# Second down pair of a decoder layer: six of eleven chunks by seven products instead of three, with two weight sums of each made by DMA

## The chip, the cores and the metric

The kernel runs on one core of one Trainium2 chip. The metric is the device time of one execution in microseconds (us), lower is better. Times shown are medians of several runs, beside the lowest and the highest; one execution was also profiled, and all rows of the trace come from that one.

## What is computed

One layer of a decoder for 256 rows of 2048 numbers, in float32. The part that matters here is the last product of the feed-forward half, from 5632 to 2048 columns:

```python
    h2 = rmsnorm(x, g_ffn)
    gu = h2 @ w_gu
    x = x + (jax.nn.silu(gu[..., :D_FF]) * gu[..., D_FF:]) @ w_down
    return x
```

In the kernel the product of silu and the second half of `gu` is called `a`; it has 256 rows and 5632 columns, and is needed transposed.

## The kernel before

**Precision.** TensorE (PE) multiplies in a format shorter than float32. Each operand is therefore split: ScalarE (ACT) casts it to a high part (`w_hi`, `a_hi`), and VectorE (DVE) subtracts that from the original and keeps the rest as a low part (`w_lo`, `a_lo`). `split` (line 108) emits the two instructions. `product` (lines 170 to 172) then issues three matmuls, high by high, high by low, low by high, each 128x128 by 128x512. So each weight tile costs one ACT and one DVE instruction of 128x1024, and then PE uses it. `w_hi` and `w_lo` have five buffers each, the raw weights `w_raw` four.

**The down product.** `a` is cut into eleven chunks of 512 columns, the output into four blocks of 512 columns, and the blocks are made two at a time: `down_pair` is called twice, and each call makes 256 rows by 1024 columns. `own` holds its four PSUM tiles (row half t, column block n). A chunk gives each of the four a contribution. Plainly done (`rest`, one call for each column block n and half of the chunk kh) this takes four weight tiles, four splits and 48 matmuls.

**By sevens.** Three of the eleven chunks (`WD`, chunks 4, 6 and 8) are done by `seven` instead: the 2x2 block product of a chunk is made from seven products of sums, in the manner of Strassen and Winograd. The four weight tiles b11, b12, b21, b22 (`g_raw`, four buffers) are summed into `u` (one buffer) and into b12, and each of the seven `form` calls splits one tile and issues 6 matmuls: 42 for the chunk instead of 48. Sums of `a` are wanted too; `sums` makes them with four small DVE steps in place, and they are split into `a_shi` and `a_slo`. Four of the seven products collect in PSUM tiles of their own (`f1`, `f5`, `f6`, `f7`, from `spare`) over all the chunks done so, and `combine` adds them to the output once per pair.

**What sets the order.** `down_pair` calls `rest` for the plain chunks in turn and takes steps of the generator `by_sevens` between them. Each split also advances the queue `stages`, which brings in the chunks of `a`: `fetch_a` (line 1028) loads a chunk from DRAM (`a_mem`) into `a_raw`, two buffers, and `take_a` splits it. The order in which the program was written is then rearranged by a scheduler while it is built, so an engine's real row of instructions is read from its order, below. At run time each engine works through its row in that order.

**Queues.** Weight loads are issued by SyncE (SP, line 291), loads of `a_raw` and of the residual by GpSimd (POOL), outputs by two queues for each pair. An earlier stage, the product with `w_gu`, already has sums that are made by DMA: line 366, `u<-g_raw`, a DMA with `accum_op` add, issued by POOL, 512 KB.

Of the kernel before, what the change touches and what calls it, by code (L numbers as in the profile page):

```python
# [9 lines left out]
F32 = mybir.dt.float32  # L10
# [3 lines left out]
ALU = mybir.AluOpType  # L14
# [4 lines left out]
P = 128  # L19
D = 2048  # L20
S = 256
NT = S // P
# [7 lines left out]
NB = 512  # L30
# [25 lines left out]
def hybrid_block(ctx: ExitStack, tc: tile.TileContext, x, w_in, w_branch, w_out, w_gu, w_down, rel_bias,  # L56
                 onehot, extra, across, factors, out):
    nc = tc.nc
# [22 lines left out]
    def pool(stack, name, side, bufs=1):  # L81
        return stack.enter_context(tc.tile_pool(name=name, bufs=bufs, side=side, reuse_waits="tile"))
# [8 lines left out]
    def half_kb(dt=F32):  # L91

        return scratch.tile([P, NB], dt, name="sc")
# [13 lines left out]
    def split(hi, lo, src, pin=False):  # L107
        for op in nc.scalar.copy(hi, src), nc.vector.tensor_sub(lo, src, hi.bitcast(F32)):  # L108
            if pin:
                tc.keep_in_program_order(op)  # L110
# [5 lines left out]
    def raw_weights(w, row0, c, col0):  # L116
        raw = wpool.tile([P, 2, NB], F32, name="w_raw", bufs=4)
        return raw, nc.sync.dma_start(raw, block(w, row0 // P + c, col0))
# [12 lines left out]
    stages, slow_stages = [], []  # L131
# [35 lines left out]
    def product(ps, ah, al, wh, wl, start=False, stop=False):  # L167
        how = dict(skip_group_check=True)
        wh, wl = woven(wh), woven(wl)
        nc.tensor.matmul(ps, ah, wh, start=start, stop=False, **how)  # L170
        nc.tensor.matmul(ps, ah, wl, start=False, stop=False, **how)  # L171
        nc.tensor.matmul(ps, al, wh, start=False, stop=stop, **how)  # L172
# [36 lines left out]
    def sums(t0, t1, pin=False):  # L209


        a11, a12, a21, a22 = (a[:, 2 * kh:2 * kh + 2, :] for a in (t0, t1) for kh in range(2))
        first = nc.vector.tensor_sub(a22, a21, a22)
        if pin:
            tc.keep_in_program_order(first)
        nc.vector.tensor_sub(a21, a11, a21)
        nc.vector.tensor_sub(a11, a22, a11)
        nc.vector.tensor_add(a12, a12, a11)
# [3 lines left out]
    class Sums:  # L222
# [19 lines left out]
        def form(self, f, c, j):  # L242
            if f in SUM_AT:
                kh, t = SUM_AT[f]
                return [x[:, 2 * kh + j, t * P:(t + 1) * P] for x in self.s[c]]
            return self.plain(*{1: (0, 4 * c + j), 2: (0, 4 * c + 2 + j), 4: (1, 4 * c + 2 + j)}[f])
# [41 lines left out]
    def load(w, k, col0, pl=None):  # L288

        raw = pl.tile([P, 2, NB], F32, name="g_raw", bufs=6 if pl is gx else 4) if pl else wpool.tile([P, 2, NB], F32, name="w_raw", bufs=4)  # L290
        (nc.sync.dma_start if w is w_down else fetch)(raw, block(w, k, col0))
        return raw

    def parts(src):
        hi = wpool.tile([P, 2, NB], F32R, name="w_hi")
        lo = wpool.tile([P, 2, NB], F32R, name="w_lo")
        split(hi, lo, src)
        advance(stages)
        split_count[0] += 1
        if split_count[0] % 2:  # L300
            advance(slow_stages)
        return hi, lo
# [3 lines left out]
    def snapshot(ps):  # L306
        sb = half_kb()
        nc.scalar.copy(sb, ps)  # L308
        return sb
# [144 lines left out]
    for k in (4, 6):  # L454
        raw, issue = raw_weights(w_in, 0, k, V0)
# [497 lines left out]
    pr = pool(ctx, "pr", "right")  # L953
# [16 lines left out]
    a_mem = dram.tile([NF // 4, P, 4, S], F32, name="a_mem")  # L970

    WD = (4, 6, 8)
    ORDER = [0, 1, 2, 4, 3, 6, 5, 8, 7, 9, 10]
    EARLY = 3
    a = Chunks(None, "a", NF // 4, WD, False)
# [88 lines left out]

    stages.append(take_rest())

    def down_pair(c0, mine, spare, queues):


        own = dict(zip(((0, 0), (1, 0), (0, 1), (1, 1)), mine()))  # L1070
        begun = set()
        xc = {}
        for t in range(NT):
            for n in range(2):
                xc[t, n] = half_kb()
                nc.gpsimd.dma_start(xc[t, n], x1[t, :, c0 + n * NB:c0 + (n + 1) * NB])

        def into(ps, lhs, wh, wl, last=False):
            for j in range(2):
                product(ps, *lhs(j), wh[:, j], wl[:, j], id(ps) not in begun, last and j == 1)  # L1080
                begun.add(id(ps))

        def rest(c, n, kh, last=False):
            k = 4 * c + 2 * kh
            wh, wl = parts(load(w_down, k, c0 + n * NB))
            for t in range(NT):
                into(own[t, n], lambda j: a.plain(t, k + j), wh, wl, last)

        def form(ps, f, c, src, last=False):
            wh, wl = parts(src)  # L1090
            into(ps, lambda j: a.form(f, c, j), wh, wl, last)

        def seven(c, f1, f5, f6, f7, last):
            def quarter(kh, n):
                return load(w_down, 4 * c + 2 * kh, c0 + n * NB, gd)

            b11 = quarter(0, 0)
            form(f1, 1, c, b11, last)
            yield
            b12 = quarter(0, 1)  # L1100
            u = gd.tile([P, 2, NB], F32, name="u", bufs=1)
            tc.keep_in_program_order(nc.vector.tensor_add(u, b11, b12))
            form(f5, 5, c, u, last)
            yield
            b22 = quarter(1, 1)
            nc.vector.tensor_add(u, u, b22)
            form(f6, 6, c, u, last)
            yield
            nc.vector.tensor_add(b12, b12, b22)
            form(f7, 7, c, b12, last)  # L1110
            yield
            form(own[0, 1], 3, c, b22)
            yield
            b21 = quarter(1, 0)
            form(own[0, 0], 2, c, b21)
            yield
            nc.vector.tensor_add(u, u, b21)
            form(own[1, 0], 4, c, u)
            yield

        def combine(f1, f5, f6, f7):

            s1 = snapshot(f1)
            nc.vector.tensor_add(xc[0, 0], xc[0, 0], s1)
            nc.vector.tensor_add(s1, f6, s1)
            s3 = half_kb()
            nc.vector.tensor_add(s3, f7, s1)
            s5 = snapshot(f5)
            yield
            nc.vector.tensor_add(xc[1, 0], xc[1, 0], s3)  # L1130
            nc.vector.tensor_sub(s1, s5, s1)
            nc.vector.tensor_add(xc[0, 1], xc[0, 1], s1)
            nc.vector.tensor_sub(s3, s5, s3)
            nc.vector.tensor_add(xc[1, 1], xc[1, 1], s3)
            yield

        def by_sevens():
            f = spare()
            for c in WD:
                yield from seven(c, *f, c == WD[-1])  # L1140
            yield from combine(*f)

        sevens = by_sevens()
        plain = [(c, n, kh) for c in ORDER if c not in WD for kh in range(2) for n in range(2)]
        for i, at in enumerate(plain[:-4]):
            rest(*at)
            if i >= 6:
                next(sevens, None)
        for _ in sevens:
            pass  # L1150
        for n in range(2):
            for kh in range(2):
                rest(plain[-1][0], n, kh, kh == 1)
            for t in range(NT):
                for half in range(2):
                    n0 = half * (NB // 2)
                    cols = slice(n0, n0 + NB // 2)
                    y = xc[t, n]
                    nc.vector.tensor_add(y[:, cols], own[t, n][:, cols], y[:, cols])
                    queues[half].dma_start(  # L1160
                        out[t * P:(t + 1) * P, c0 + n * NB + n0:c0 + n * NB + n0 + NB // 2], y[:, cols])
# [4 lines left out]
    def elsewhere():  # L1166
        return [acc2.tile([P, NB], F32, name=n) for n in "zv"] + [tr.tile([P, NB], F32, name="tr") for _ in range(2)]

    down_pair(0, in_acc, elsewhere, (nc.scalar, nc.gpsimd))
    down_pair(2 * NB, elsewhere, in_acc, (nc.scalar, nc.sync))  # L1170


_INS = ["x", "w_in", "w_branch", "w_out", "w_gu", "w_down", "rel_bias"]
# [33 lines left out]
```

## Time and profile before

| | us |
|---|---|
| median of 3 runs (lowest, highest) | 1344.98 (1343.92, 1347.02) |
| profiled execution, its own time | 1344.12 |
| its span in the trace | 1342.4 |
| PE busy | 1333.9 |
| DVE busy | 1154.9 |
| ACT busy | 917.4 |
| POOL busy | 118.0 |

The span goes from the first instruction to the last; the execution's own time is a little longer. Busy time is the sum of the stretches in which an engine worked on an instruction. The records of matmuls overlap, so that the distance between the starts of two of them is the time that one takes.

### The profile page before, as it was taken

What the parts mean: (1) busy time and instruction counts of PE and PEld (TensorE: products, weight loads), DVE (VectorE), ACT (ScalarE), POOL (GpSimd) and SP (SyncE); (2) the same over time, 40 slices, a digit from 0 to 9 for tenths busy, and PEclk for the clock granted to TensorE, in tenths of its full rate; (3) what the DMA queues carried; (4) which work ended last, traced back from release to release, by engine and by line L of the source; (5) the groups of instructions that cost most, each with busy time, mean ns of one, the idle gap of its engine ahead of it and who ended that gap; (6) DMA issues with size and microseconds to landing.
All of it is one profiled execution on the core that took longest, in us unless ns stands there. A gap on an engine that the chain in (4) does not pass through costs nothing.

```text
span 1342.4 us, 17715 instructions
## 1 busy us (share of the span) xinstructions
PE 1333.9 (99%) x6266; PEld 1165.2 (87%) x6266; DVE 1154.9 (86%) x1239; ACT 917.4 (68%) x1175; POOL 118.0 (9%) x180
## 2 busy tenths in 40 slices
PE   9999999999999999999999999999999999999998
PEld 6888888888888888888888888888888888888887
DVE  7988898988889996876689999999999997996785
ACT  7786967888776775445567778777877876664453
POOL 1100010101110112100100000001000001000000
PEclk9999999999999999999999999999999999999999
DMA  9987877888788878977788989899999987787652
GB/s 361 305 282 248 268 208 246 269 255 244 250 276 278 268 241 286 309 232 223 238 325 258 269 250 282 222 263 302 289 281 284 245 240 254 251 307 239 204 186 96
DMA packets 117200, 346.83 MB, mean 258 GB/s; under 512 B 32576, under 2 KB 34296, under 8 KB 117112
## 3 DMA queue, kind: packets, MB, share of 16 engines
q1 hardware_dynamic: 76872, 277.45, 59.6%
q0 software_dynamic: 17824, 61.90, 19.7%
q10 hardware_dynamic: 22416, 6.36, 2.8%
q8 instruction: 49, 0.80, 0.2%
q14 instruction: 39, 0.32, 0.1%
HBM read 293.21 MB, written 14.70 MB: 229 GB/s over the span
## 4 chain that ended last, share of the span: by engine, by line
PE 96%; DVE 2%; ACT 1%; issue 0%; DMA 0%; SPq 0%; DVEq 0%; ACTq 0%
PE qs L171 12%; PE qs L170 12%; PE qs L172 12%; PE ps L171 12%; PE ps L172 12%; PE ps L170 12%; PE z L170 4%; PE z L171 4%; PE z L172 4%; PE v L171 2%; PE v L172 2%; PE v L170 2%; PE tr L172 1%; PE tr L170 1%; PE tr L171 1%; PE tr L192 1%
## 5 line engine op out<-in xcount | busy, mean ns | idle before, releaser
L108 DVE TENSOR_TENSOR w_lo<-w_raw,w_hi 128x1024 fp32r<-128x1024 f32 x318 | 386.9, 1221 | 86.2 <-ACT w_hi L108 84.6
L108 ACT CAST w_hi<-w_raw 128x1024 fp32r<-128x1024 f32 x318 | 331.8, 1048 | 142.9 <-PE qs L172 49.3
L108 ACT CAST w_hi<-g_raw 128x1024 fp32r<-128x1024 f32 x200 | 207.5, 1049 | 131.8 <-PE qs L172 37.1
L108 DVE TENSOR_TENSOR w_lo<-g_raw,w_hi 128x1024 fp32r<-128x1024 f32 x200 | 238.7, 1221 | 29.6 <-ACT w_hi L108 28.0
L108 ACT CAST w_hi<-u 128x1024 fp32r<-128x1024 f32 x150 | 155.4, 1047 | 79.7 <-PE ps L172 20.7
L108 DVE TENSOR_TENSOR w_lo<-u,w_hi 128x1024 fp32r<-128x1024 f32 x150 | 180.6, 1221 | 32.9 <-ACT w_hi L108 29.9
L171 PE MATMUL qs<-w_lo,h_hi 128*128 128x512 f32 x348 | 132.7, 381 | 0.0
L172 PE MATMUL qs<-w_hi,h_lo 128*128 128x512 f32 x348 | 132.2, 380 | 0.0
L171 PE MATMUL ps<-w_lo,h_hi 128*128 128x512 f32 x336 | 128.1, 382 | 0.2 <-DVE w_lo L108 0.2
L172 PE MATMUL ps<-w_hi,h_lo 128*128 128x512 f32 x336 | 127.5, 380 | 0.1
L170 PE MATMUL qs<-w_hi,h_hi 128*128 128x512 f32 x348 | 125.0, 382 | 0.0
L170 PE MATMUL ps<-w_hi,h_hi 128*128 128x512 f32 x336 | 121.1, 382 | 0.0
L170 PEld LDWEIGHTS qs<-w_hi,h_hi 128*128 128x128 f32 x348 | 65.9, 189 | 9.4 <-ACT sc L308 0.4
L171 PEld LDWEIGHTS qs<-w_lo,h_hi 128*128 128x128 f32 x348 | 65.9, 189 | 9.1
L172 PEld LDWEIGHTS qs<-w_hi,h_lo 128*128 128x128 f32 x348 | 65.9, 189 | 9.1
L172 PEld LDWEIGHTS ps<-w_hi,h_lo 128*128 128x128 f32 x336 | 63.6, 189 | 9.7 <-DVE h_lo L108 1.1
L171 PEld LDWEIGHTS ps<-w_lo,h_hi 128*128 128x128 f32 x336 | 63.6, 189 | 9.6 <-DVE w_lo L108 1.1
L170 PEld LDWEIGHTS ps<-w_hi,h_hi 128*128 128x128 f32 x336 | 63.4, 190 | 8.9 <-ACT h_hi L108 0.3
L366 POOL DMA_DIRECT2D u<-g_raw x44 | 38.2, 868 | 363.6 <-DVE w_lo L108 252.5
L324 DVE TENSOR_TENSOR u<-g_raw 128x1024 f32<-128x1024 f32 x44 | 53.6, 1220 | 7.7 <-DMA g_raw<-in_w_gu 5.8
L313 DVE TENSOR_TENSOR u<-u,g_raw 128x1024 f32<-128x1024 f32 x44 | 51.8, 1218 | 0.0
L171 PE MATMUL z<-w_lo,h_hi 128*128 128x512 f32 x104 | 39.5, 380 | 0.0
(400 smaller groups left out, 2956.5 us busy)
## 6 DMA issues: line engine op xcount, KB each, us to landing
w_raw<-in_w_in SPq DMA_DIRECT2D x104, 512.0 KB, 6.8
g_raw<-in_w_in SPq DMA_DIRECT2D x88, 512.0 KB, 6.5
g_raw<-in_w_gu SPq DMA_DIRECT2D x88, 512.0 KB, 6.2
w_raw<-in_w_gu SPq DMA_DIRECT2D x88, 512.0 KB, 7.4
w_raw<-in_w_down SPq DMA_DIRECT2D x64, 512.0 KB, 4.3
u<-g_raw POOLq DMA_DIRECT2D x44, 512.0 KB, 6.9
w_raw<-in_w_branch SPq DMA_DIRECT2D x32, 512.0 KB, 4.9
w_raw<-in_w_out SPq DMA_DIRECT2D x32, 512.0 KB, 4.4
```

What stands on the lines that cost most here:

```text
L108: for op in nc.scalar.copy(hi, src), nc.vector.tensor_sub(lo, src, hi.bitcast(F32)):
L170: nc.tensor.matmul(ps, ah, wh, start=start, stop=False, **how)
L171: nc.tensor.matmul(ps, ah, wl, start=False, stop=False, **how)
L172: nc.tensor.matmul(ps, al, wh, start=False, stop=stop, **how)
L192: nc.tensor.transpose(pt[:, i, :], src[:, i * P:(i + 1) * P], ident)
L313: tc.keep_in_program_order(nc.vector.tensor_add(d, d, a))
L324: nc.vector.tensor_add(d, a, b)
L366: nc.gpsimd.dma_start(d, a, accum_op=ALU.add)
```

## The change

The first pair stays as it is. In the second pair chunks 3, 5 and 7 are also done by sevens, after 4, 6 and 8. Their sums of `a` aren't there, so `sums_again` loads each chunk once more from `a_mem`, sums it and splits the result into the room of the plain chunks 0, 1 and 2, which are done by then. Two of the four sums of weights in each seven (`b12 += b22` and `u += b21`) are made by DMA instead of DVE, for which form 7 moves behind forms 3 and 2. The steps of the sevens begin with the first plain step of the pair instead of the seventh, 2.75 of them after each plain step.

```diff
+    def sums_again(c, room):
+        raw = pr.tile([P, 4, S], F32, name="a_raw", bufs=2)
+        nc.gpsimd.dma_start(raw, a_mem[c])
+        for _ in range(4):
+            yield
+        sums(*(raw[:, :, t * P:(t + 1) * P] for t in range(NT)), True)
+        yield
+        split(*a.t[room], raw, True)
+        a.s[c] = a.t[room]
+        yield
...
             b22 = quarter(1, 1)
             nc.vector.tensor_add(u, u, b22)
+            if by_dma:
+                nc.gpsimd.dma_start(b12, b22, accum_op=ALU.add)
             form(f6, 6, c, u, last)
             yield
-            nc.vector.tensor_add(b12, b12, b22)
-            form(f7, 7, c, b12, last)
-            yield
+            if not by_dma:
+                nc.vector.tensor_add(b12, b12, b22)
+                form(f7, 7, c, b12, last)
+                yield
             form(own[0, 1], 3, c, b22)
             yield
             b21 = quarter(1, 0)
+            if by_dma:
+                nc.gpsimd.dma_start(u, b21, accum_op=ALU.add)
             form(own[0, 0], 2, c, b21)
             yield
-            nc.vector.tensor_add(u, u, b21)
+            if by_dma:
+                form(f7, 7, c, b12, last)
+                yield
+            else:
+                nc.vector.tensor_add(u, u, b21)
             form(own[1, 0], 4, c, u)
...
-        plain = [(c, n, kh) for c in ORDER if c not in WD for kh in range(2) for n in range(2)]
+        plain = [(c, n, kh) for c in ORDER if c not in sevenths for kh in range(2) for n in range(2)]
+        done, first = 0, 0 if again else 6
+        rate = (7 * len(sevenths) + 2) / (len(plain) - 4) if again else 1
         for i, at in enumerate(plain[:-4]):
             rest(*at)
-            if i >= 6:
+            if at[0] in again and at[1:] == (1, 1):
+                stages.append(sums_again(again[at[0]], at[0]))
+            while i >= first and done < (i - first + 1) * rate:
                 next(sevens, None)
+                done += 1
...
-    down_pair(2 * NB, elsewhere, in_acc, (nc.scalar, nc.sync))
+    down_pair(2 * NB, elsewhere, in_acc, (nc.scalar, nc.sync), WD + (3, 5, 7), True, {0: 3, 1: 5, 2: 7})
```

The order of instructions moves with it. First DVE, in the second pair, from the first sum `u` of the second seven on (chunk 6). Before, its row reads:

```order
L1102 TENSOR_TENSOR u_11525<-g_raw_11493,g_raw_11523 128x1024
L1109 TENSOR_TENSOR g_raw_11523<-g_raw_11523,g_raw_11555 128x1024
L108 TENSOR_TENSOR w_lo_11528<-u_11525,w_hi_11527 128x1024
L108 TENSOR_TENSOR w_lo_11540<-w_raw_11537,w_hi_11539 128x1024
L1106 TENSOR_TENSOR u_11525<-u_11525,g_raw_11555 128x1024
L108 TENSOR_TENSOR w_lo_11559<-u_11525,w_hi_11558 128x1024
L108 TENSOR_TENSOR w_lo_11571<-w_raw_11568,w_hi_11570 128x1024
L1117 TENSOR_TENSOR u_11525<-u_11525,g_raw_11643 128x1024
```

The changed kernel's DVE row at the same place, on to form 4 (the split of `u_11309` for the third time; `w_lo_11397` is form 7):

```order
L1113 TENSOR_TENSOR u_11309<-g_raw_11295,g_raw_11307 128x1024
L108 TENSOR_TENSOR w_lo_11312<-u_11309,w_hi_11311 128x1024
L108 TENSOR_TENSOR w_lo_11324<-w_raw_11321,w_hi_11323 128x1024
L1117 TENSOR_TENSOR u_11309<-u_11309,g_raw_11339 128x1024
L108 TENSOR_TENSOR w_lo_11344<-u_11309,w_hi_11343 128x1024
L108 TENSOR_TENSOR w_lo_11356<-g_raw_11339,w_hi_11355 128x1024
L108 TENSOR_TENSOR w_lo_11368<-w_raw_11365,w_hi_11367 128x1024
L108 TENSOR_TENSOR w_lo_11387<-g_raw_11383,w_hi_11386 128x1024
L108 TENSOR_TENSOR w_lo_11397<-g_raw_11307,w_hi_11396 128x1024
L213 TENSOR_TENSOR a_raw_11347<-a_raw_11347 128x2x128
L108 TENSOR_TENSOR w_lo_11411<-u_11309,w_hi_11410 128x1024
```

The sum at line 1109 is gone from behind the first sum, whose split now follows it at once, and so is the sum at line 1117 of the before kernel, ahead of form 4; the small sums of `a` have come in between.

Second POOL, in the second pair, in the changed kernel: the sums by DMA (lines 1119 and 1130), the outputs of the first pair (1185) and a reload of `a_raw` (1069) stand in one row. None of the rows of lines 1119, 1130 and 1069 was there before.

```order
L1119 DMA g_raw_11188<-g_raw_11202 128x1024
L1185 DMA out_0<-sc_10176 128x256
L1185 DMA out_0<-sc_10180 128x256
L1185 DMA out_0<-sc_10178 128x256
L1185 DMA out_0<-sc_10182 128x256
L1130 DMA u_11190<-g_raw_11244 128x1024
L1119 DMA g_raw_11307<-g_raw_11339 128x1024
L1130 DMA u_11309<-g_raw_11383 128x1024
L1119 DMA g_raw_11452<-g_raw_11466 128x1024
L1069 DMA a_raw_11766<-a_mem_6325 128x1024
L1130 DMA u_11454<-g_raw_11508 128x1024
```

So the sums of one seven by DMA alternate with those of the next, one at a time, where DVE had them.

## Rows read from the trace of the kernel before

**Rows 1.** The page: span, and each engine's busy time, share and instructions.
```profile
span 1342.4 us, 17715 instructions
...
PE 1333.9 (99%) x6266; PEld 1165.2 (87%) x6266; DVE 1154.9 (86%) x1239; ACT 917.4 (68%) x1175; POOL 118.0 (9%) x180
```

**Rows 2.** Timeline of PE where the second pair begins and ends: start, us, instruction.
```profile
1228.06 0.38 PE L170 MATMUL z<-w_hi,a_hi 128*128 128x512 f32 x1
...
1337.92 0.38 PE L172 MATMUL tr<-w_hi,a_lo 128*128 128x512 f32 x1
```

**Rows 3.** Stretches: w_gu product, first down pair, second down pair until its tail.
```profile
core 0: us, PE busy (x) PEld busy (x) DVE busy (x) ACT busy (x) POOL busy (x), PEclk, DMA share, GB/s
930.00:1060.00 130.00, 130.00 (x604) 114.04 (x603) 121.42 (x114) 97.13 (x108) 11.57 (x14) 1.00 0.94 263
1120.00:1228.00 108.00, 108.00 (x505) 94.51 (x504) 100.64 (x108) 67.46 (x74) 7.90 (x14) 1.00 0.79 264
1228.00:1331.60 103.60, 103.60 (x482) 90.89 (x481) 78.75 (x74) 52.05 (x51) 1.08 (x2) 1.00 0.56 177
```

**Rows 4.** Waits in the second pair, 1228 to 1338 us, the longest in total.
```profile
DVE w_lo L108 <- ACT w_hi L108: 21.2, 21, 1.4
ACT w_hi L108 <- PE v L172: 15.1, 12, 1.6
ACT w_hi L108 <- PE tr L172: 13.4, 13, 1.5
ACT w_hi L108 <- DVE u L1102: 7.5, 3, 2.5
```

**Rows 5.** Timeline of DVE in the second pair; in brackets idle time before, and releaser.
```profile
1269.34 1.22 DVE L1102 TENSOR_TENSOR u<-g_raw 128x1024 f32<-128x1024 f32 x1
1270.59 1.23 DVE L1109 TENSOR_TENSOR g_raw<-g_raw 128x1024 f32<-128x1024 f32 x1
1271.75 1.23 DVE L108 TENSOR_TENSOR w_lo<-u,w_hi 128x1024 fp32r<-128x1024 f32 x1
1272.89 1.22 DVE L108 TENSOR_TENSOR w_lo<-w_raw,w_hi 128x1024 fp32r<-128x1024 f32 x1
1274.03 1.22 DVE L1106 TENSOR_TENSOR u<-u,g_raw 128x1024 f32<-128x1024 f32 x1
1276.45 1.23 DVE L108 TENSOR_TENSOR w_lo<-u,w_hi 128x1024 fp32r<-128x1024 f32 x1 [1.20 <-ACT w_hi L108]
...
1317.00 0.68 DVE L1131 TENSOR_TENSOR sc<-sc 128x512 f32<-128x512 f32 x1
1317.60 0.68 DVE L1133 TENSOR_TENSOR sc<-sc 128x512 f32<-128x512 f32 x1
```

**Rows 6.** Timeline of DVE in the first pair, at a small sum of a.
```profile
1175.15 0.42 DVE L213 TENSOR_TENSOR a_raw<-a_raw 128x256 f32<-128x256 f32 x1
1175.49 1.22 DVE L108 TENSOR_TENSOR w_lo<-w_raw,w_hi 128x1024 fp32r<-128x1024 f32 x1
```

**Rows 7.** Timeline of ACT, the cast of the sum made at 1274.03.
```profile
1275.36 1.06 ACT L108 CAST w_hi<-u 128x1024 fp32r<-128x1024 f32 x1 [2.70 <-DVE u L1106]
```

**Rows 8.** Timelines of DVE and POOL in the w_gu product, at one accumulate.
```profile
1088.84 2.36 DVE L108 TENSOR_TENSOR w_lo<-u,w_hi 128x1024 fp32r<-128x1024 f32 x2 [0.39 <-ACT w_hi L108]
...
1090.36 0.90 POOL L366 DMA_DIRECT2D u<-g_raw  x1 [20.12 <-DVE w_lo L108]
```

**Rows 9.** Line 366, all 44 accumulates of the w_gu and w_in products, issue to landing.
```profile
DMA to landing us min/median/max: 4.4/6.9/11.4
```

**Rows 10.** Line 366 at 410, 818, 974, 1051 and 1090 us, first of two.
```profile
DMA to landing us min/median/max: 4.5/4.5/4.5
...
DMA to landing us min/median/max: 5.8/5.8/5.8
...
DMA to landing us min/median/max: 6.1/6.1/6.1
...
DMA to landing us min/median/max: 8.6/8.6/8.6
...
DMA to landing us min/median/max: 5.1/5.1/5.1
```

**Rows 11.** DMA queue of POOL: packets, MB, share of 16 engines' span.
```profile
q0 software_dynamic: 17824, 61.90, 19.7%
```

**Rows 12.** DMA issues by line: count, KB each, median us from issue to landing.
```profile
g_raw<-in_w_down SPq DMA_DIRECT2D x24, 512.0 KB, 4.8
g_raw<-g_raw POOLq DMA_DIRECT2D x18, 512.0 KB, 7.8
...
a_raw<-a_mem POOLq DMA_DIRECT2D x8, 512.0 KB, 5.5
```

**Rows 13.** Timeline of DVE where the first pair's last results leave PSUM.
```profile
1227.95 1.41 DVE L1159 TENSOR_TENSOR sc<-qs,sc 128x256 f32<-128x256 f32 x4
```

More of the change, by code (lines that the diff above doesn't have):

```diff
@@ L1065, in hybrid_block, with down_pair @@
     stages.append(take_rest())
-    def down_pair(c0, mine, spare, queues):
+    def sums_again(c, room):
[8 more added lines that the diff above has]
+        yield
+    def down_pair(c0, mine, spare, queues, sevenths, by_dma=False, again={}):
         own = dict(zip(((0, 0), (1, 0), (0, 1), (1, 1)), mine()))
@@ L1138, in by_sevens @@
             f = spare()
-            for c in WD:
-                yield from seven(c, *f, c == WD[-1])
+            for c in sevenths:
+                yield from seven(c, *f, c == sevenths[-1])
             yield from combine(*f)
         sevens = by_sevens()
-        plain = [(c, n, kh) for c in ORDER if c not in WD for kh in range(2) for n in range(2)]
+        plain = [(c, n, kh) for c in ORDER if c not in sevenths for kh in range(2) for n in range(2)]
+        done, first = 0, 0 if again else 6
+        rate = (7 * len(sevenths) + 2) / (len(plain) - 4) if again else 1
         for i, at in enumerate(plain[:-4]):
             rest(*at)
-            if i >= 6:
+            if at[0] in again and at[1:] == (1, 1):
+                stages.append(sums_again(again[at[0]], at[0]))
+            while i >= first and done < (i - first + 1) * rate:
                 next(sevens, None)
+                done += 1
         for _ in sevens:
@@ L1167, in elsewhere @@
         return [acc2.tile([P, NB], F32, name=n) for n in "zv"] + [tr.tile([P, NB], F32, name="tr") for _ in range(2)]
-    down_pair(0, in_acc, elsewhere, (nc.scalar, nc.gpsimd))
-    down_pair(2 * NB, elsewhere, in_acc, (nc.scalar, nc.sync))
+    down_pair(0, in_acc, elsewhere, (nc.scalar, nc.gpsimd), WD)
+    down_pair(2 * NB, elsewhere, in_acc, (nc.scalar, nc.sync), WD + (3, 5, 7), True, {0: 3, 1: 5, 2: 7})
 _INS = ["x", "w_in", "w_branch", "w_out", "w_gu", "w_down", "rel_bias"]
```

## Prediction

> **What bounds the kernel now.** The page comes first: TensorE (PE) is busy in 1333.9 of 1342.4 us [rows 1], so time is won only by taking matmuls away, and lost wherever PE is made to wait. The stretches say how near the others are. The second down pair, the one stage that the change touches, runs from 1228.06 us, when its first matmul starts [rows 2], to the last one at 1337.92. It holds 510 matmuls by the code (eight plain chunks of 48, three by sevens of 42): 109.9 us for 509 steps, 0.216 us each. In it VectorE (DVE) is busy 78.75 of 103.6 us, the DMA engines 0.56 of the time; in the first pair DVE has 100.64 of 108 us and PE still never waits [rows 3]. The waits of the stage are DVE's and ScalarE's (ACT) upon each other and ACT's for PE to free a weight buffer [rows 4]; none is PE's. So PE leads here with five buffered pairs of weights behind it, and the question is whether DVE, in its fixed order, can still feed it.
>
> **What is removed.** Three chunks go from 48 to 42 matmuls, 18 in all: 18 x 0.216 = 3.9 us. That is all the change can win. Weight loads stay at 44.
>
> **What DVE is asked for.** One weight split or sum of 128x1024 steps by 1.135 us where DVE is packed (1271.75 to 1272.89 [rows 5]); a small sum of 128x256 by 0.34 us (1175.15 to 1175.49 [rows 6]); a combine step of 128x512 by 0.60 [rows 5]. A chunk by sevens wants 7 splits and, now, 2 sums: 10.2 us against PE's 9.1; a plain one 4.5 against 10.4. Added per new chunk are also four small sums and one split, 2.5 us, three times. Taken together that fits, but the order does not let it be taken together.
>
> I count from the end of form 6's split in the second seven (chunk 6) to the end of the same in the last one (chunk 7). Between them the changed DVE order has 49 large instructions, 12 small and one of 512: 49 x 1.135 + 12 x 0.34 + 0.6 = **60.3 us**. PE has 28 forms and 10 rests there, 288 matmuls, 62.1 us. PE's start is better by a lead: form 6 is wanted after 4 rests and 9 forms, 102 x 0.216 = 22.0 us from 1228.06, at 1250.1. DVE gets there as follows. Form 1 of the same seven takes the eleventh pair of buffers of this stage; there are five, so its cast waits until PE is through with the sixth, 48 matmuls in, at 1238.4. From there a cast (1.05 and some 0.1), six large DVE steps (form 1, sum, form 5, a plain split, sum, form 6) and two waits of 1.2 us (below) end at 1248.9. PE also runs two matmuls that need only the high parts before it meets the low one (0.4 us, from PE's order). Lead 1.6 us; PE can cover **63.7 us**.
>
> **First added wait: the cast.** A sum made by DVE must be cast by ACT before DVE can split it. Before, u += b22 at 1274.03 was followed by 1.20 us of idle DVE until the cast, begun at 1275.36, was done [rows 5, 7]; the first sum had no such hole, since b12 += b22 stood behind it. That filler is what the change takes out of DVE, so now both sums have one. From the new order, less what still stands between: 0.85 + 1.2 (third seven), 1.2 + 1.2, 0.1 + 1.2, 0.5 + 0.6: **6.85 us**.
>
> **Second added wait: the accumulate.** u += b21 was one DVE step; now GpSimd (POOL) issues it after form 6's split is done, and ACT's cast and DVE's split for form 4 wait for its landing, with the whole rest of both engines queued behind them. The way there: split's end to issue 0.3 (1088.84 plus 1.22 to 1090.36 [rows 8]); landing L; then 0.1, the cast 1.05, 0.1: L + 1.55 us. What DVE does meanwhile, from its order, in the second to fifth seven: 4.88, 5.68, 5.56, 5.68 us. For L the same instruction, same size, stands in the earlier stage: 4.4 to 11.4, median 6.9 [rows 9]; but there two are issued together, and here one. Looked at alone, the first of a pair landed after 4.5, 5.8, 6.1, 8.6 and 5.1 us [rows 10]. The traffic here is lighter to begin with (0.56 against 0.94 of the engines in that stage [rows 3]); added are twelve accumulates and three reloads of 0.52 MB, at 61.90 MB for 19.7% of the span [rows 11], 2.2 us each, 34 us, which brings it to about 0.88 by my estimate. I take **L = 5.5**, between the quiet and the middle ones: holes of 2.17, 1.37, 1.49, 1.37 = **6.4 us**.
>
> A rule of the Trainium skill prices the same transfer otherwise. Its page DMA: Bandwidth & Descriptors, section Anatomy of one DMA — SWDGE (gpsimd) path, gives such a DMA about 2.0 us and its bytes at 436 GB/s; for 512 KB that is an estimate of 3.2 us. By it the holes would be nil and the sum -0.5 us instead of +6.0. No accumulate in this trace landed that fast, so the rows decide.
>
> **Sum.** 60.3 + 6.85 + 6.4 = 73.6 against 63.7: PE is late by 9.9 us at the last form 6, less 3.9 saved: **+6.0 us**. With holes(L) it is holes - 0.5: +1.5 at L = 4.4, +11.5 at 6.9, +18 at 8.6.
>
> **What costs nothing.** The remaining parts hide while DVE is the late one. The other accumulate, b12 += b22, is issued when u is made and b22 is there, and form 7 wants it 7 large steps and two casts' waits later, 10.3 us in the second seven; with the 7.8 us of the row of that kind [rows 12], the same 0.3 before it and the cast behind it, 9.4. It hides, by little. b12's next load is freed by form 3's split, b22's by the accumulate's landing; both have 7 us or more before their sums, and loads of this kind take 4.8 [rows 12]. The reloads of a_raw (5.5 us [rows 12]) are asked for a chunk ahead. The sevens' early start meets the first pair's drain: form 6's split stands behind a drain that PE frees at 1227.95 [rows 13] and ends near 1230.6, wanted at 1233.2. The tail (four rests, then output) is unchanged.
>
> **Rivals.** (1) Contention: the accumulates fall among loads, L nears 6.9 and above: +11.5, about 1356.5. For it: 0.88 busy engines, the 8.6 among the rows. The Trainium skill's same page, Issuing engines are not separate DMA queues, says that all issuers share 16 engines and interleave; a median of 6.9 [rows 9] with the engines 0.94 busy doesn't speak against it. Against the rival: here they come one at a time. Chance 0.2. (2) No change: L at 4.4 to 4.7, the best rows: +1.5, 1346.5. Chance 0.2. By the formula of the Trainium skill above it would end here too. (3) Faster: the buffers hold PE. Five pairs are worth up to five times 1.65 us; if form 6's split in the second seven is ready not 1.6 but about 10 us ahead, no wait of the sum reaches PE, and the 3.9 us come through: 1341.1. For it: DVE's bare work, 60.3, is under 63.7, and the first pair hides all with DVE at 93%. Against: the pair now begins with sevens at once, and the eleventh buffer is bound to the sixth. Break-even is that split done at about 1243 instead of 1248.9. Chance 0.15. My own case, L from 4.7 to 6.3, +3 to +9: 0.45.
>
> **Numbers.** The sum stands against the profiled execution, 1344.12 us; the median of three is 1344.98, 0.9 above. So 1350.1 profiled, and **1351.0** as a median. The range takes in (2) and most of (1), and a part of (3): 1342 to 1358; the likeliest case alone is 1348 to 1354. Within 0.2% (2.7 us), what a measurement here can tell: 0.2; faster 0.15; slower 0.65.
>
> **What would show it.** PE idle 8 to 11 us in the second pair, most of it before form 6 of the third, fifth and sixth sevens (u, psum qs), released by DVE's w_lo; DVE idle of about 1.2 us after each new sum; ACT waiting for the accumulate on u once a chunk, for about 1 to 3 us; DVE near 90% busy there. I am wrong if PE has no idle time there (3), if the accumulates land under 4.6 us (2), if ACT waits for b12's accumulate or for loads instead, or if the granted clock falls below the 1.00 of [rows 3], for which this trace has no price.

## The result, and the profile after

| | before | changed |
|---|---|---|
| median of 6 runs each, us | 1345.18 | 1355.08 |
| lowest and highest | 1343.92, 1347.46 | 1352.17, 1362.63 |
| profiled execution, its own time | 1344.12 | 1352.94 |
| its span | 1342.4 | 1351.2 |

The changed kernel is slower: the ratio of the times is 1.0077, with a 95% interval of 1.0049 to 1.0105, or +9.9 us at the median and +8.8 us between the two profiled spans. 1351.0 was predicted. The direction was right and the range held; the size was too small by 4 us, and the likeliest case's own range (1348 to 1354) just missed. The profiled execution is the second fastest of its six; the two longest, 1358.12 and 1362.63, show a mean granted clock of TensorE of 0.996 and 0.997 over the span, the other four 0.999.

The page of the changed kernel, where it answers to [rows 1] and [rows 11]: span, busy time of the engines, POOL's DMA queue.

```profile
span 1351.2 us, 17782 instructions
PE 1335.7 (99%) x6248; PEld 1160.7 (86%) x6248; DVE 1171.2 (87%) x1263; ACT 926.5 (69%) x1187; POOL 130.1 (10%) x195
q0 software_dynamic: 19984, 69.76, 22.8%
```

PE reads 99% again, though it has 18 matmuls fewer and the span is longer: a share of the whole span hides 9 us. The stretches of the second pair don't (columns as in [rows 3]):

```profile
1228.00:1250.00 22.00, 22.00 (x104) 19.28 (x102) 15.94 (x16) 11.85 (x13) 2.84 (x4) 1.00 0.94 275
1250.00:1270.00 20.00, 16.18 (x69) 12.43 (x67) 15.46 (x17) 10.00 (x12) 2.26 (x3) 0.97 0.83 234
1270.00:1290.00 20.00, 20.00 (x86) 16.94 (x87) 15.89 (x17) 11.62 (x12) 2.58 (x3) 0.94 0.86 247
1290.00:1310.00 20.00, 18.09 (x80) 14.60 (x80) 17.86 (x18) 11.76 (x12) 1.71 (x2) 1.00 0.88 231
1310.00:1330.00 20.00, 18.00 (x81) 14.83 (x80) 17.42 (x20) 10.27 (x11) 1.71 (x2) 1.00 0.74 218
```

Read the counts of matmuls, not only the busy time: 20 us hold 92.7 matmuls at full rate, and here there are 69 to 86. In the third row PE is busy all the time with 86: its granted clock was below 1.00. DVE, the engine that makes PE wait, is idle in every row.

Over the whole pair (first and last matmul in PE's timeline):

```profile
1227.98 0.38 PE L170 MATMUL z<-w_hi,a_hi 128*128 128x512 f32 x1
...
1346.88 0.38 PE L172 MATMUL tr<-w_hi,a_lo 128*128 128x512 f32 x1
```

The first matmul starts at 1227.98 us, the last at 1346.88, 118.90 us. At the step of before (109.86 us for 509 steps, 0.2158) 491 steps take 105.97. So 12.9 us are lost and 3.9 saved. The difference of 9.0 is that of the spans, 8.8, within 0.2: hardly anything outside of the second pair has a part in it.

Where PE waits, in the third seven (chunk 8), in PE's timeline; form 6 is the row with qs:

```profile
1266.50 0.38 PE L172 MATMUL ps<-w_hi,a_slo 128*128 128x512 f32 x1
1268.96 0.80 PE L170 MATMUL qs<-w_hi,a_shi 128*128 128x512 f32 x1 [2.08 <-ACT w_hi L108]
1269.91 0.80 PE L170 MATMUL z<-w_hi,a_hi 128*128 128x512 f32 x1 [0.15 <-ACT w_hi L108]
1270.49 0.63 PE L170 MATMUL v<-w_hi,a_hi 128*128 128x512 f32 x1
1270.92 0.63 PE L171 MATMUL qs<-w_lo,a_shi 128*128 128x512 f32 x1
1271.35 0.64 PE L172 MATMUL qs<-w_hi,a_slo 128*128 128x512 f32 x1
```

And DVE's timeline around it:

```profile
1261.85 1.22 DVE L1113 TENSOR_TENSOR u<-g_raw 128x1024 f32<-128x1024 f32 x1
1262.99 0.42 DVE L218 TENSOR_TENSOR a_raw<-a_raw 128x256 f32<-128x256 f32 x1
1264.26 1.22 DVE L108 TENSOR_TENSOR w_lo<-u,w_hi 128x1024 fp32r<-128x1024 f32 x1 [0.85 <-ACT w_hi L108]
1265.40 1.22 DVE L108 TENSOR_TENSOR a_lo<-a_raw,a_hi 128x1024 fp32r<-128x1024 f32 x1
1266.54 1.22 DVE L1117 TENSOR_TENSOR u<-u,g_raw 128x1024 f32<-128x1024 f32 x1
1268.94 1.23 DVE L108 TENSOR_TENSOR w_lo<-u,w_hi 128x1024 fp32r<-128x1024 f32 x1 [1.19 <-ACT w_hi L108]
...
1277.54 1.23 DVE L108 TENSOR_TENSOR w_lo<-u,w_hi 128x1024 fp32r<-128x1024 f32 x1 [1.70 <-ACT w_hi L108]
```

The second sum ends at 1267.76, ACT casts it, and only at 1268.94 may DVE go on: 1.19 us idle, as in [rows 5], and now behind both sums. The last idle time shown, 1.70 us before form 4's split, looks the same in DVE's row, but ACT's wait behind it is for the accumulate. The waits of the stage, 1226 to 1350 us, name it (total, times, longest):

```profile
DVE w_lo L108 <- ACT w_hi L108: 20.1, 17, 2.5
ACT w_hi L108 <- DMA u<-g_raw: 16.4, 6, 3.8
ACT w_hi L108 <- DVE u L1113: 14.9, 5, 3.5
ACT w_hi L108 <- DVE u L1117: 12.8, 5, 2.7
...
PE qs L170 <- ACT w_hi L108: 4.3, 3, 2.1
...
ACT w_hi L108 <- DMA w_raw<-in_w_down: 1.7, 1, 1.7
```

The last of these rows is the only wait of ACT for a weight load, and it stands at 1337.43 us, in the tail; DVE and PE wait for none. So late loads are not what holds the changed kernel up.

From issue to landing the six accumulates on u took (line 1130; below it the first seven's alone, which was issued while four output DMAs of the first pair were under way):

```profile
DMA to landing us min/median/max: 4.7/5.8/8.2
...
DMA to landing us min/median/max: 8.2/8.2/8.2
```

### The profile page after: what moved, and what is told of

Same layout as the page of the kernel before. It is cut to its first block, busy times and chain, and to the rows that moved or that the text cites. A ratio compares the mean times of both kernels' runs of the same rounds, so it can differ in the third digit from the quotient of the medians.

```text
span 1351.2 us, 17782 instructions
## 1 busy us (share of the span) xinstructions
PE 1335.7 (99%) x6248; PEld 1160.7 (86%) x6248; DVE 1171.2 (87%) x1263; ACT 926.5 (69%) x1187; POOL 130.1 (10%) x195
## 4 chain that ended last, share of the span: by engine, by line
PE 91%; DVE 3%; DMA 3%; issue 2%; ACT 1%; SPq 0%; POOL 0%; DVEq 0%; ACTq 0%; POOLq 0%
PE qs L171 12%; PE qs L172 12%; PE qs L170 12%; PE ps L171 12%; PE ps L172 12%; PE ps L170 12%; PE z L170 3%; PE z L171 3%; PE z L172 3%; PE v L171 2%; PE v L172 2%; PE v L170 2%; DVE w_lo L108 2%; DMA u<-g_raw 1%; ACT w_hi L108 1%
## 5 line engine op out<-in xcount | busy, mean ns | idle before, releaser
L108 DVE TENSOR_TENSOR w_lo<-w_raw,w_hi 128x1024 fp32r<-128x1024 f32 x306 | 371.7, 1219 | 79.5 <-ACT w_hi L108 78.9
L108 ACT CAST w_hi<-w_raw 128x1024 fp32r<-128x1024 f32 x306 | 318.8, 1047 | 127.6 <-PE qs L172 43.7
L108 ACT CAST w_hi<-g_raw 128x1024 fp32r<-128x1024 f32 x212 | 219.5, 1049 | 119.3 <-PE qs L172 39.5
L108 DVE TENSOR_TENSOR w_lo<-g_raw,w_hi 128x1024 fp32r<-128x1024 f32 x212 | 253.1, 1219 | 23.0 <-ACT w_hi L108 21.6
L108 ACT CAST w_hi<-u 128x1024 fp32r<-128x1024 f32 x159 | 164.6, 1046 | 113.3 <-DVE u L1113 25.7
L108 DVE TENSOR_TENSOR w_lo<-u,w_hi 128x1024 fp32r<-128x1024 f32 x159 | 191.4, 1220 | 47.3 <-ACT w_hi L108 44.3
L172 PE MATMUL v<-w_hi,h_lo 128*128 128x512 f32 x104 | 39.4, 379 | 0.0
```

## The experiments

The theory, T: DVE's order makes PE late, by a wait for the cast behind each sum and a hole until the accumulate has landed, while its work alone would fit. The rivals: R_work, the amount of DVE's work binds in any order; R_dma, the accumulates and reloads slow the transfers that feed the engines. All kernels were compared with the kernel before on the same chip. "Lost" is worked out as above from each profiled run: the pair's length less its matmuls at 0.2158 us.

| kernel | difference of medians, us | ratio, 95% interval | pair, us | lost, us |
|---|---|---|---|---|
| changed | +9.9 | 1.0077 [1.0049, 1.0105] | 118.90 | 12.9 |
| e1_dve_sums | +8.6 | 1.0068 [1.0054, 1.0082] | 119.12 | 13.2 |
| e2_b12_dma_only | +5.8 | 1.0042 [1.0030, 1.0054] | 115.31 | 9.3 |
| e3_three_by_dma | -0.2 | 1.0001 [0.9993, 1.0010] | 109.86 | 0 |
| e4_four_sevens | -1.1 | 0.9983 [0.9975, 0.9992] | 108.56 | 0 |
| e5_no_accumulate | +1.8 | 1.0017 [1.0003, 1.0032] | 110.62 | 4.7 |
| e6_two_u | +5.2 | 1.0031 [1.0019, 1.0043] | 114.98 | 9.0 |
| e7_two_u_late4 | +20.8 | 1.0156 [1.0137, 1.0176] | 129.04 | 23.1 |
| e8_late4_more_raw | -3.2 | 0.9977 [0.9968, 0.9986] | 106.47 | 0.5 |
| e9_first_by_dve | +9.3 | 1.0068 [1.0055, 1.0081] | 119.80 | 13.8 |
| e10_after_again | +10.0 | 1.0069 [1.0055, 1.0083] | 118.79 | 12.8 |

**The accumulate on u left out** (e5).

```diff
             b21 = quarter(1, 0)
-            if by_dma:
-                nc.gpsimd.dma_start(u, b21, accum_op=ALU.add)
             form(own[0, 0], 2, c, b21)
```

> The changed kernel without u += b21 (form 4 multiplies u without b21, so that term of the products is left out of the output); VectorE, ScalarE and TensorE have the same instructions in the same order, and the accumulate on b12 stays. Theory T: no hole before form 4's split: 60.3 + 6.85 = 67.2 against 63.7, less 3.9: -0.5 to +0.5 us to the kernel before, 8 to 9 us faster than the changed kernel. R_work: VectorE's work is the same, so it stays at +9. R_dma: half the accumulates gone, +4 to +5.

Of the changed kernel's +9.9 us 1.8 are left, with every DVE, ACT and PE instruction in place. R_work falls. R_dma expected +4 to +5, and the interval reaches to +4.3, so this run alone does not exclude it. T's upper end, +0.5, is passed by 1.3 at the median and by 0.3 in the profiled pair (110.62 to 109.86). In the pair 4.7 of the 12.9 us lost are left.

**All sums on DVE again** (e1, the first piece), and **only the one on u** (e2, the second).

```diff
-    down_pair(2 * NB, elsewhere, in_acc, (nc.scalar, nc.sync), WD + (3, 5, 7), True, {0: 3, 1: 5, 2: 7})
+    down_pair(2 * NB, elsewhere, in_acc, (nc.scalar, nc.sync), WD + (3, 5, 7), False, {0: 3, 1: 5, 2: 7})
...
             b21 = quarter(1, 0)
-            if by_dma:
-                nc.gpsimd.dma_start(u, b21, accum_op=ALU.add)
             form(own[0, 0], 2, c, b21)
             yield
             if by_dma:
                 form(f7, 7, c, b12, last)
                 yield
-            else:
-                nc.vector.tensor_add(u, u, b21)
+            nc.vector.tensor_add(u, u, b21)
             form(own[1, 0], 4, c, u)
```

> All four sums of each of the six sevens are made by VectorE again, with no accumulating DMA in the second pair; the number of sevens and the reloads of a_raw stay. Theory T (VectorE's fixed order makes TensorE late: cast waits behind back-to-back sums, and holes until an accumulate lands): counted as in the prediction, 69.4 us of bare work and 3.7 us of cast waits (b12 += b22 fills the hole after u += b22 again) against 63.7, less 3.9: about +5.5 us to the kernel before, that is some 3 us faster than the changed kernel, though it gives VectorE 13.6 us more work. Rival R_work (the mere amount of VectorE's work binds): slower than the changed kernel, by 5 to 11 us (+14 to +20 to the kernel before). Rival R_dma (the accumulates slow the weight loads, VectorE isn't late by itself): the saving comes through, -3.9 us.

> Only b12 += b22 is left to the DMA; u += b21 is made by VectorE again, behind form 7's split, so no split for form 4 waits for a landing. Theory T: the holes of 6.4 us go, 4.5 us of work and half a cast wait come back: 64.85 + 6.16 = 71.0 against 63.7, less 3.9: about +3.4 us to the kernel before, 5 us faster than the changed kernel. R_work: slower than the changed kernel by about 4.5 us. R_dma (half the accumulates gone): somewhere halfway between the kernel before and the changed one, +2 to +5, so this run alone doesn't tell it from T.

e1 gives DVE 13.6 us more work and is no slower than the changed kernel: R_work, +14 to +20, falls, and so does R_dma, -3.9, since without any accumulate nothing comes through. T's +5.5 is missed by 3.1 as well. Its window does better than its total: form 6's split ends 21.61 us after the pair's start in the second seven (20.84 by the prediction), and 74.26 us later in the last one (73.1 expected), which makes PE late by 9.4 + 0.77 + 1.16 = 11.3 of the 13.15 us lost. The other 1.8 come behind the last form 6, and the granted clock shows them (stretches of e1; the column before the last two):

```profile
1318.00:1322.00 4.00, 3.18 (x14) 2.14 (x12) 4.00 (x7) 1.70 (x3) 0.00 (x0) 1.00 0.15 61
1322.00:1326.00 4.00, 2.96 (x7) 2.43 (x8) 3.97 (x4) 4.00 (x5) 0.00 (x0) 0.64 0.01 2
1326.00:1330.00 4.00, 4.00 (x18) 3.40 (x18) 4.00 (x5) 2.88 (x4) 0.00 (x0) 0.93 0.26 67
```

Form 6 at 1323.04 had begun 1.25 us late, for the cast, and the matmuls right behind it took some 1.8 us more than as many at full rate. T had no term for that. e2 behaves as T says in sign and order (2.4 us above its +3.4, 4 us better than the changed kernel though DVE has more to do), which R_work can't explain; R_dma's +2 to +5 is no farther off, as was said of this run beforehand.

**Three and four sevens, by DMA** (e3, e4).

```diff
-    down_pair(2 * NB, elsewhere, in_acc, (nc.scalar, nc.sync), WD + (3, 5, 7), True, {0: 3, 1: 5, 2: 7})
+    down_pair(2 * NB, elsewhere, in_acc, (nc.scalar, nc.sync), WD, True)
...
+    down_pair(2 * NB, elsewhere, in_acc, (nc.scalar, nc.sync), WD + (3,), True, {0: 3})
```

> Three sevens as before, no sums made anew and no reloads, begun with the first rest and spread over the pair; two sums of each by accumulating DMA as in the changed kernel. Theory T: three sevens among eight plain chunks leave VectorE far ahead, so cast waits and holes (about 6 us in all) lie in its spare time: within 1 us of the kernel before. R_dma: the accumulates themselves cost, half as many of them: +3 to +5 us. R_work: no change.

> Four sevens instead of six (one chunk's sums made anew in the room of a plain chunk, one reload), accumulating DMAs as in the changed kernel. Theory T: VectorE has some 10 us more to spare over the pair than with six, so casts and holes are hidden, and the 6 matmuls taken out come through: -1.3 us to the kernel before, at worst 0. R_dma (the accumulates slow the loads): two thirds of the changed kernel's loss, +4 to +7. R_work: no loss either, so this run tells T from R_dma alone.

In e3, unlike what its expectation says, the sevens begin with the seventh plain step and go on one step at a time, as in the kernel before: its edit gives no chunks to sum anew, and the earlier start hangs on those. So it changes the two sums alone. Both came as T has them: no change, and -1.1 for six matmuls (1.3). Their accumulates on u landed no sooner than the changed kernel's (median 5.9 and 6.4 us), and PE waited for nothing in either. The pair's stretch of e4:

```profile
1228.00:1337.00 109.00, 109.00 (x507) 95.39 (x505) 80.91 (x82) 55.76 (x55) 7.08 (x9) 1.00 0.70 217
```

**A second buffer for the sums** (e6).

```diff
             b22 = quarter(1, 1)
-            nc.vector.tensor_add(u, u, b22)
+            nc.vector.tensor_add(b11 if by_dma else u, u, b22)
+            if by_dma:
+                u = b11
             if by_dma:
                 nc.gpsimd.dma_start(b12, b22, accum_op=ALU.add)
```

> The second sum of a seven, u += b22, is written into b11's buffer instead of over u, so VectorE can make both sums back to back and the first one's cast and split fall behind the second; the same instructions, sums, DMAs and matmuls otherwise. Theory T: the cast waits shrink from 6.9 to some 0.6 us, the holes before form 4's split stay: about +2.5 to +3 us to the kernel before (the changed kernel: +9.9). R_work: the work is the same, +9. R_dma: the DMAs are the same, +9.

The sums now stand back to back and the waits for their casts are gone, and the kernel gains 4.7 us on the changed one with the same work: against R_work and R_dma. The holes stayed, and grew: 2.22, 2.44, 0.72 and 2.87 us of idle DVE before form 4's split. T expected a gain of 7. The rest has a place of its own: before form 5 of the last seven PE waits for the new sum of a (PE's timeline of e6):

```profile
1315.51 0.38 PE L172 MATMUL tr<-w_hi,a_lo 128*128 128x512 f32 x1
1319.07 0.69 PE L170 MATMUL ps<-w_hi,a_hi 128*128 128x512 f32 x1 [3.19 <-ACT a_hi L108]
```

The four small sums of `sums_again` stand in DVE's row behind form 4's split, before which DVE had stood idle for those 2.87 us. Behind PE's wait eight matmuls ran slow again, 1.7 us more. I had counted those sums as work and not as something PE could wait for.

**Form 4 put off** until after form 5 of the next seven (e7), and the same with **b22 and b21 in w_raw** (e8).

```diff
             def quarter(kh, n):
-                return load(w_down, 4 * c + 2 * kh, c0 + n * NB, gd)
+                return load(w_down, 4 * c + 2 * kh, c0 + n * NB, None if by_dma and kh else gd)
...
             form(f5, 5, c, u, last)
             yield
+            if late:
+                form(own[1, 0], 4, *late.pop())
+                yield
             b22 = quarter(1, 1)
...
-            form(own[1, 0], 4, c, u)
-            yield
+            if by_dma and not last:
+                late.append((c, u))
+            else:
+                form(own[1, 0], 4, c, u)
+                yield
...
+        late = []
```

The first piece is e8's alone; both have the second buffer of e6.

> As the kernel with two buffers for the sums, and form 4 put off until after form 5 of the next seven, so that its accumulate has some 11 us to land. Theory T: neither cast waits nor holes before form 4's split (-3.9 if that were all), but b11's buffer is held some 10 us longer and the four raw buffers run short: the load of the next b12 waits for the accumulate, 2.7 us a seven by the order. So between -2 and +3, and any idle time of TensorE ends with a load of a g_raw tile, not with the accumulate. R_work and R_dma: +9.

> As the kernel with form 4 put off, with b22 and b21 loaded into the four buffers of the plain loads, so that the four g_raw buffers serve b11 and b12 alone. Theory T: VectorE's bare 59.7 us against some 62 of TensorE, cast waits 0.1 each, no holes, no shortage of buffers: the saving comes through, -3.9 us to the kernel before (1341), at worst -2. R_work: same work as the changed kernel, +9. R_dma: the same DMAs, +9.

e7 is the largest miss: +20.8 where at most +3 was expected, though with the cause named, loads of g_raw. First an accumulate, the loads behind it, and DVE's sum that waits for one of them (timelines of POOL, SP's queue and DVE), then two rows of the stage's waits:

```profile
1250.88 0.88 POOL L1135 DMA_DIRECT2D g_raw<-g_raw  x1 [6.30 <-DMA g_raw<-in_w_down]
...
1251.27 0.33 SPq L291 DMA_DIRECT2D w_raw<-in_w_down  x1
1259.46 0.80 SPq L291 DMA_DIRECT2D g_raw<-in_w_down  x2
1260.31 0.42 SPq L291 DMA_DIRECT2D w_raw<-in_w_down  x1
...
1263.07 1.23 DVE L1113 TENSOR_TENSOR u<-g_raw 128x1024 f32<-128x1024 f32 x1 [4.46 <-DMA g_raw<-in_w_down]
...
POOL g_raw L1135 <- DMA g_raw<-in_w_down: 31.1, 5, 9.6
...
SPq L291 <- DMA g_raw<-g_raw: 25.1, 6, 7.7
```

The accumulate lands 8.5 us after its issue, at 1259.4; SP's next load wants a buffer that it holds and leaves at 1259.46; and SP takes its loads in order, so that one for w_raw stands behind it. The late load then makes DVE's sum late, and the next accumulate too. I had priced one load a seven, not the row behind it, and not that the delay comes round again.

With the four w_raw buffers in use too, the shortage is gone: e8 is 3.2 us faster than the kernel before, which puts it 13 us ahead of the changed one. The second pair of e8 and of the changed kernel, as stretches:

```profile
1228.00:1335.00 107.00, 106.89 (x496) 92.96 (x494) 95.85 (x102) 62.53 (x63) 11.09 (x14) 1.00 0.84 245
```

```profile
1228.00:1347.00 119.00, 111.28 (x493) 92.85 (x491) 95.66 (x101) 61.87 (x64) 11.10 (x14) 0.99 0.77 220
```

This pair of rows settles it between T and the two rivals. DVE has 95.85 and 95.66 us of work, ACT 62.5 and 61.9, the DMA engines are busier in the faster kernel (0.84 to 0.77), and its accumulates land no sooner (line 1135 of e8, those on the second buffer):

```profile
DMA to landing us min/median/max: 5.1/6.4/7.6
```

What differs is the order, what stands between a sum and the split that needs it, and the room for the raw tiles. The room alone was not run apart, but in the changed kernel it had nothing to mend: no engine there waits for a load before the tail.

**The first seven's accumulate on DVE** (e9), beside the changed kernel once more (e10).

```diff
-            if by_dma:
+            if by_dma and c != sevenths[0]:
                 nc.gpsimd.dma_start(u, b21, accum_op=ALU.add)
...
-            else:
+            if not by_dma or c == sevenths[0]:
                 nc.vector.tensor_add(u, u, b21)
```

> The changed kernel with u += b21 of the first seven alone made by VectorE; the other five by DMA as they are. Theory T with the lead as the mis-sized term (the first seven's accumulate landed after 8.25 us beside the output DMAs, so form 4's split came 2.42 us late and form 6's split of the second seven ended level with TensorE instead of 1.6 us ahead): the split ends some 1.2 us earlier, the last form 6 too, so the second pair is 1.2 us shorter than the changed kernel's. Rival (the start doesn't matter, the loss all arises later): no difference.

> The changed kernel once more, beside the run above on the same chip: +8.5 to +10.5 us to the kernel before. Its second pair is as late as VectorE's order and the landings make it, whichever they are this time: idle time and slower steps of TensorE less 3.9 us give the difference of the spans.

e9 did not get clearly shorter: +9.3 beside +10.0, intervals alike, and its profiled pair is 1.0 us longer than e10's. That decides nothing between the expectation and its rival, because the two ended up with nearly the same lead. In e9 form 6's split of the second seven ended 21.34 us after the start, 1.1 sooner than in the changed kernel's first profile (22.41), about as expected; but in e10, with nothing changed, the first accumulate landed after 7.0 us instead of 8.2, and that split ended at 21.13. There the last form 6 began 1.42 us sooner than in the first profile; yet as much was lost, because PE then ran at the lower clock (stretches, e10 first, then the changed kernel's first profile):

```profile
1322.00:1326.00 4.00, 2.80 (x7) 2.12 (x8) 3.44 (x4) 4.00 (x5) 0.86 (x1) 0.65 0.12 25
```

```profile
1322.00:1326.00 4.00, 2.40 (x9) 1.47 (x10) 3.44 (x4) 2.95 (x4) 0.35 (x1) 1.00 0.19 38
```

From the start of the last form 6 to the last matmul it is 24.05 us in e10 and 24.06 in e9, and 22.73 in the first profile. What makes e9's pair longer than e10's lies between: it has a hole of 1.45 us in the fourth seven, where e10 has 0.66 (landings after 5.28 and 4.72 us).

## Why the prediction was right, and too small

**What bounds, and the mechanism: right.** DVE's fixed order, with two added waits, makes PE late in the second pair and nowhere else. e5 takes away one wait, e6 the other, e8 both at the same work, and in e8 all but 0.5 us of the 12.9 lost are back.

**The saving: right.** 3.9 us expected; e8 shows them less that half microsecond, e4 a third of them.

**The cast waits: right.** 6.85 us expected; DVE's idle times of that kind in the first profile add up to 6.6 (four of 1.19, and 0.85, 0.40, 0.56 and less).

**The accumulate's holes: right.** L = 5.5 expected, and the second to fifth seven's landed after 5.90, 5.91, 4.93 and 5.78; holes of 2.50, 1.70, 0.86 and 1.58 make 6.6 where 6.4 stood. The sum hung on this term most, and the single rows of the earlier stage [rows 10] were the right ones to take. The Trainium skill's page DMA: Bandwidth & Descriptors, section Anatomy of one DMA — SWDGE (gpsimd) path, by which I had estimated 3.2 us, doesn't agree with this trace: none of the twelve accumulates landed under 4.66 us.

**The bare work: mis-sized.** 60.3 us expected, 61.8 found (74.96 us between the two splits less 13.2 of idle time). Every step was taken as packed, 1.135 us; but an instruction ahead of idle time takes its full 1.22, as the sum at 1266.54 does in the rows above. With eleven such places that is 0.9 us of the 1.5; the rest is in single steps of 1.26 us where 1.135 was counted, and its cause stays open.

**The lead: the term that was most mis-sized.** I had 1.6 us, counted from the buffers alone. For the first seven I checked form 6 against the drain and never priced its accumulate; in the first profile it landed after 8.2 us, DVE stood idle for 2.42 us before form 4's split, and ended form 6's split of the second seven at 22.41 us instead of 20.84, 1.6 us later than I had it. With the bare work that is the whole of the difference in this run: 9.9 + 1.6 + 1.4 = 12.9 us lost (1.4 for the whole stretch between the two splits, 74.96 us where the sum has 73.55). The same count holds for the other two profiles, with other terms. In e10 the lead is only 0.3 us short, the stretch 1.3 us longer than the sum, and 1.3 are the slow matmuls behind the last form 6: 12.8. In e9, with the accumulate gone, it is 0.5, 2.1 and 1.3: 13.8. So the lead was wrong for the profiled run, but the loss doesn't hang on it alone; it was partly chance that so different terms came to so similar totals.

**The clock: not priced.** The prediction put it among what would make it wrong, and it did fall below 1.00: 0.97 and 0.94 in two of the stretches above. By the arithmetic above it cost nothing in the first profile, where the slow matmuls fell ahead of another wait for DVE, and 1.3 us in e10 and e9, where they fell behind the last wait. How much of the median's +9.9 it is can't be said: only two executions of the changed kernel were profiled, 1352.94 and 1352.85 us where the medians are 1355.08 and 1356.13, and its runs spread over 10 us.

**The rivals.** The contention rival had said 1356.5, nearer to the median than my 1351.0, and was still wrong: its busy engines came (0.85 from 1228 to 1331.6 us, for my estimate of 0.88), but its L of 6.9 didn't, save for the first seven's 8.2, and e8 has as many accumulates with a loss of 0.5 us, e3 and e4 half and two thirds of them with none. No change (L at 4.4 to 4.7) fell with the landings. Faster, by the buffers, fell by the idle time of PE.

**What would show it.** PE's waits stand before form 6 of the third, fifth and sixth sevens, as said, with shorter ones elsewhere. I named DVE's w_lo as their releaser; it is ACT's w_hi, since the first matmul of a form needs the high part alone and comes as soon as that is cast. PE's idle time is 7.7 us (111.28 busy of 119.00), a little under the 8 to 11 that I named: a matmul that runs alone is recorded with more than its step, and slow steps count as busy. ACT's waits for the accumulate were 2.3 to 3.8 us, for 1 to 3. DVE near 90% busy was wrong by my own terms: 60.3 of 73.6 is 82%, and 83.17 of 103.6 us (80%) is what the stretch of [rows 3] shows now.

## What to carry to other kernels

Where engines work through fixed rows, count what stands between the maker of a value and its reader, not only the sum of the work: a sum that is cast by another engine before it is split costs that cast as idle time unless something is put between. A DMA that takes a step off a busy engine only helps if its landing is covered in that engine's row; and a buffer that it reads is held until it lands, so the room for the next loads has to grow with the cover. Price the first round of a changed loop apart, since the stage before it still has transfers under way.

## What the runs showed of the hardware

**A short wait can cost twice.** After waits of PE of 1 to 3 us the granted clock fell in some places and not in others. In the first profile's rows above, the matmuls from 1270.49 on start 0.43 us apart, where the packed step is 0.216: the lower of the two levels, 1.2 GHz for 2.4. The Trainium skill's page TensorE: Matmul & The Clock Gate, section Back-to-back issue gap, has formulas for the step of an isolated matmul at the two levels, by which I estimate 0.427 and 0.216 us for 512 columns, and the trace agrees. The 0.131 us that the same section gives for a sustained stream of such matmuls doesn't agree with this trace: the 509 steps of the kernel before took 0.2158 each. In e1 and e10 a delay of about 1.3 us at the last form 6 goes with a granted clock of 0.64 and 0.65 from 1322 to 1326 us, in the changed kernel's first profile the same delay at the same place with 1.00. What PE had done just before differs little between the last two (another delay of 0.7 us, 2.3 us ahead in both); what decides it was not found.

**An accumulate of 512 KB within SBUF** took 4.4 to 9.2 us from issue to landing in the second pair of these runs. It was not quicker in the kernels with fewer of them (median of all 6.1 us in e3, 6.4 in e4, 5.9 in the changed kernel), nor slower in e8 with its busier engines (5.9); over all kernels these medians go from 5.1 (e6) to 7.2 (e2), and what moves them was not found.
